# Late projections at every third round and output splits one per round, in the HGRN and attention stage of a hybrid decoder layer

## The chip, the cores and the metric

The kernel runs on one core of a Trainium2 chip. The metric is the device time of one execution, in microseconds (us); the time before is the median of 3 runs.

## The reference

One decoder layer over a sequence of 1024 tokens with width 1024, in float32. Features are kept as 8 blocks of 128 partitions, tokens along the free axis. Cut to what matters:

```python
def layer(h):
    a = rmsnorm(h) @ W_in                     # 30 blocks of 128 columns
    h = h + concat(hgrn2(a), dilated_window_mix(a), rwkv7(a)) @ W_out
    h = h + gated_mlp_with_causal_conv3(rmsnorm(h))
    h = h + sigmoid(rmsnorm(h) @ W_g) * (p @ W_p)
    return rmsnorm(h)

# hgrn2, four heads of 128: S_t = diag(f_t) S_{t-1} + (1 - f_t) i_t^T, o_t = S_t^T q_t,
#   then o * rsqrt(mean(o*o) + eps) * g * silu(gate)
# dilated_window_mix, four heads of 64: softmax attention over three dilated windows,
#   combined by their softmax denominators
# rwkv7, four heads of 64
```

## The kernel before

A float32 product is done as three matmuls of split operands, xh·whi + xl·whi + xh·wlo (`mm3`), where hi is the value rounded for TensorE's fast mode and lo is what is left. A weight block of 1024 columns is loaded, cast on ScalarE (whi, line 114) and subtracted on VectorE or GpSimd (wlo, line 116). `dense` runs the 8 blocks of the inner dimension through `mm3`.

The layer runs as stages: the norm, the RWKV heads in two pairs, then HGRN and attention together, the output projection, the MLP, the gate and the last norm. The engines' instruction order is static: a scheduler takes the instructions as the Python code issues them, with priorities, and writes one list for each engine.

The change touches the stage of HGRN and attention, which `phase_mix` writes. It interleaves five generators by a string of letters:

- A: HGRN heads 0 and then 2; B: HGRN heads 1 and then 3 (`handover`: the second begins when the first is 14 steps in).
- C: the attention (`swa`), two pairs of heads p of eight query blocks each: scores (swq on PE), mask and minimum (lg and sden on DVE), exponential on ACT, transposes (swt), values (swo) and their copy into the output tile ob.
- F: the late projections (`project_late`).
- M: what is left of the RWKV work.

There are 36 rounds. In each A has a turn, B from the sixth on, C in the rounds of `TURNS`, and F in the rounds of `LATE` (line 344). F has four blocks of W_in to project, 29, 18, 22 and 23, each in two halves of 512 tokens. A half is 24 matmuls of 128x512 into a PSUM tile zp, followed by its finish (the row scale at line 320, for some a sigmoid at line 460 and a product at line 462 into the tile zst) and a store to DRAM. The halves are called half 1 to half 8 below. When all are done, the buffers of the normalized input X are free, since nothing reads it any more: `project_late` takes tiles in the same buffers for the input of the output projection (`self.O`), and calls `o_split` for each block k in `self.done`, in one turn. A split is two casts on ScalarE (xh, line 160) and two subtractions (xl, line 162), the first half on DVE and the second on POOL. The blocks in `done` are 6, 7 (RWKV), 0, 1 (HGRN heads that have ended) and 4 (attention pair 0); blocks that come later are split by their own streams.

An HGRN head computes its scores by levels: a score matmul (hsc, line 989) gives what DVE selects into hS (line 991), DVE then rescales qt (line 1002), POOL or DVE rescales hk (line 1000), ACT copies ks (line 976), and the next level's hsc reads qt and ks. When a head ends, its output is squared and summed (hss, line 1066), POOL raises the sum to the power −0.5 (hrs, line 1069), DVE scales ho (line 1071), and PE transposes it (vt, line 1077).

Buffers that matter: the PSUM pool "mx" has four (zp, vt, swt, swo and hsc share it); the PSUM pool for scores has two (swq); zst has two, of which the attention's output tile ob of pair 0 holds one until it is split; the tag "sslot" of the attention's pool has four.

Of the kernel before, what the change touches and what calls it, by code (L numbers as in the profile page):

```python
# [10 lines left out]
F32 = mybir.dt.float32  # L11
# [7 lines left out]
P = 128  # L19
T = 1024  # L20
# [45 lines left out]
def interleave(order, streams):  # L66

    live = dict(streams)
    while live:
        for s in order:  # L70
            if s in live and next(live[s], STOP) is STOP:
                del live[s]
# [17 lines left out]
class Trunk:  # L90
# [231 lines left out]
    def phase_mix(self):  # L322
# [8 lines left out]
        with tc.tile_pool(name="hg", bufs=1) as slots, tc.tile_pool(name="sw", bufs=1) as sp:  # L331
# [8 lines left out]
            for r in range(36):  # L340
                order += "C" * (r in self.TURNS) + "A" + "B" * (r > 5) + "F" * (r in self.LATE)
            interleave(order, {"A": A, "B": B, "C": self.swa(sp), "F": self.project_late(self.rest), "M": self.more})

    LATE = (1, 3, 6, 9, 12, 15, 18, 20, 21)

    TURNS = [i * 33 // 22 for i in range(1, 23)]

# [116 lines left out]
    def project_late(self, js):  # L464


        nc = self.nc
        for j in js:
            w = self.load_w(self.a["w_in"][j])
            t = self.keep.tile([P, T], F32, tag="zst", name=self.nm("zst"), bufs=2)  # L470
            d = self.zpool.tile([P, T], F32, tag=f"z{j}", name=f"z{j}")
            kind = (j - 8) % 4 if j < 24 else 2
            turn = j < 24 and kind < 3
            for hf in (0, 1):
                ps = self.mxp.tile([P, HT], F32, tag="mx", name=self.nm("zp"))
                self.dense({hf: ps}, w, self.X, ND, halves=(hf,))
                dst = slice((hf ^ turn) * HT, ((hf ^ turn) + 1) * HT)
                r = self.R[:, hf * HT:(hf + 1) * HT]
                self.finish(kind, t[:, dst], *((ps[:, ::-1], r[:, ::-1]) if turn and hf else (ps, r)))
                nc.sync.dma_start(d[:, dst], t[:, dst])  # L480
                if hf:
                    self.z[j] = d
                yield
        self.O = self.xall()
        for k in self.done:
            self.o_split(k)

    def zload(self, j, pool_slot, eng=None):
        t = pool_slot("zl")
        (eng or self.nc.sync).dma_start(t, self.z[j])  # L490
        return t
# [680 lines left out]
    def swa_values(self, sp, d, qb, den, pT):  # L1172
        nc = self.nc
        if qb == 0:
            d["o"] = self.keep.tile([P, T], F32, tag="zst", name=self.nm("ob"), bufs=2)
        o = d["o"]
        po = self.mxp.tile([P, P], F32, tag="mx", name=self.nm("swo"))

        for kb in range(qb + 1):
            for h, hs in enumerate(self.HEADS):  # L1180
                nc.tensor.matmul(po[hs, :], d["V"][:, kb, hs], pT[h][:, kb * P:(kb + 1) * P], start=kb == 0, stop=kb == qb)
        nc.scalar.copy(o[:, qb * P:(qb + 1) * P], po)
        if qb % 4 == 3:
            nc.vector.reciprocal(den[:, :8], den[:, :8])
            return d, qb, o, den
# [627 lines left out]
```

## Time and profile before

| what | value |
|---|---|
| median of 3 runs | 1435.65 us (1434.49 to 1436.31) |
| profiled execution | 1436.1 us |
| its span | 1434.3 us |
| its mean granted TensorE clock | 0.989 |
| instructions | 22340 |
| HBM read, written | 119.76 MB, 46.40 MB |

The span is the time from the first to the last instruction of the profiled execution; 1.8 us of that execution lie outside it. Busy shares are shares of the span. In a timeline row stand the start, the duration, the engine, the line, the operation, the names of output and inputs, sizes, how many instructions were put together in the row, and in brackets the idle time of the engine before the row with what ended it. In a row of waits stand the total, the count and the longest. The granted clock is 1.00 at full speed.

### The profile page before, as it was taken

What the parts mean: (1) busy time and instruction counts of PE and PEld (TensorE: products, weight loads), DVE (VectorE), ACT (ScalarE), POOL (GpSimd) and SP (SyncE); (2) the same over time, 40 slices, a digit from 0 to 9 for tenths busy, and PEclk for the clock granted to TensorE, in tenths of its full rate; (3) what the DMA queues carried; (4) which work ended last, traced back from release to release, by engine and by line L of the source; (5) the groups of instructions that cost most, each with busy time, mean ns of one, the idle gap of its engine ahead of it and who ended that gap; (6) DMA issues with size and microseconds to landing.
All of it is one profiled execution on the core that took longest, in us unless ns stands there. A gap on an engine that the chain in (4) does not pass through costs nothing.

```text
span 1434.3 us, 22340 instructions
## 1 busy us (share of the span) xinstructions
PE 1392.4 (97%) x8642; PEld 1124.6 (78%) x8642; DVE 1063.9 (74%) x1629; ACT 603.6 (42%) x1015; POOL 391.7 (27%) x286
## 2 busy tenths in 40 slices
PE   8999999999999989999999999999999999999996
PEld 6768777777777867787788888888888888888885
DVE  7596353964657777458888888988898799777675
ACT  7411323123145475244544444344344444455542
POOL 5221011210122231121245445445453000002331
PEclk9999999999999999999999999999999999999998
DMA  6124111240442211652413232333223963451343
GB/s 219 45 81 118 61 50 56 81 119 31 153 141 104 84 50 46 241 192 96 147 74 111 96 110 96 110 110 110 101 98 134 351 235 105 122 148 45 133 158 114
DMA packets 80122, 167.61 MB, mean 117 GB/s; under 512 B 19984, under 2 KB 22288, under 8 KB 80016
## 3 DMA queue, kind: packets, MB, share of 16 engines
q1 hardware_dynamic: 66496, 146.52, 30.2%
q10 hardware_dynamic: 12656, 16.52, 3.3%
q0 software_dynamic: 864, 3.15, 0.6%
q8 instruction: 68, 1.11, 0.3%
q14 instruction: 38, 0.31, 0.1%
HBM read 119.76 MB, written 46.40 MB: 116 GB/s over the span
## 4 chain that ended last, share of the span: by engine, by line
PE 47%; issue 3%; DVE 2%; POOL 1%; ACT 1%; DMA 0%; POOLq 0%; ACTq 0%; DVEq 0%
PE bg L1300 16%; PE bv L1300 12%; PE bv L1594 7%; PE bg L1594 7%; PE dp L141 1%; PE dp L137 1%; PE dp L139 1%; POOL wlo L116 1%; PE bv L137 0%; PE bv L139 0%; PE bv L141 0%; DVE h L1690 0%; POOL xh L162 0%; ACT whi L114 0%; DVE gt L1689 0%
## 5 line engine op out<-in xcount | busy, mean ns | idle before, releaser
L137 PE MATMUL dp<-xh,whi 128*128 128x512 f32 x544 | 191.0, 411 | 6.2 <-DVE r L500 2.9
L139 PE MATMUL dp<-xl,whi 128*128 128x512 f32 x544 | 183.7, 397 | 0.5 <-DVE xl L411 0.5
L141 PE MATMUL dp<-xh,wlo 128*128 128x512 f32 x544 | 181.8, 395 | 0.0
L116 POOL TENSOR_TENSOR wlo<-wraw,whi 128x512 fp32r<-128x512 f32 x60 | 81.7, 1363 | 326.3 <-ACT whi L114 259.7
L116 POOL TENSOR_TENSOR wlo<-raw,whi 128x512 fp32r<-128x512 f32 x84 | 134.7, 1622 | 76.1 <-ACT whi L114 76.1
L114 ACT CAST whi<-wraw 128x512 fp32r<-128x512 f32 x120 | 73.0, 617 | 165.2 <-PE dp L139 113.1
L1300 PE MATMUL bg<-t,whi 128*128 128x512 f32 x352 | 133.2, 389 | 0.0
L137 PEld LDWEIGHTS dp<-xh,whi 128*128 128x128 f32 x544 | 100.2, 190 | 35.2 <-issue 6.8
L139 PEld LDWEIGHTS dp<-xl,whi 128*128 128x128 f32 x544 | 103.0, 190 | 24.0 <-DVE xl L411 1.0
L141 PEld LDWEIGHTS dp<-xh,wlo 128*128 128x128 f32 x544 | 103.3, 190 | 23.3 <-issue 0.8
L116 POOL TENSOR_TENSOR wlo<-s,whi 128x512 fp32r<-128x512 f32 x44 | 64.2, 1460 | 174.6 <-ACT whi L114 174.6
L1594 PE MATMUL bg<-t,whi 128*128 128x512 f32 x308 | 95.2, 390 | 0.0
L1594 PE MATMUL bv<-t,whi 128*128 128x512 f32 x308 | 94.8, 389 | 0.0
L114 ACT CAST whi<-raw 128x512 fp32r<-128x512 f32 x88 | 52.6, 619 | 94.6 <-issue 48.5
L114 ACT CAST whi<-s 128x512 fp32r<-128x512 f32 x66 | 38.9, 620 | 121.1 <-PE bg L1300 113.3
L1300 PEld LDWEIGHTS bg<-t,whi 128*128 128x128 f32 x352 | 66.0, 188 | 13.7
L190 POOL TENSOR_TENSOR rst<-rst,mhalf 128x4 f32<-128x4 f32 (+1 forms) x9 | 9.9, 1102 | 235.6 <-DVE rst L186 218.6
L1594 PEld LDWEIGHTS bv<-t,whi 128*128 128x128 f32 x308 | 57.8, 188 | 12.0
L1300 PE MATMUL bg<-t,wlo 128*128 128x512 f32 x176 | 67.2, 389 | 0.0
L1594 PEld LDWEIGHTS bg<-t,whi 128*128 128x128 f32 x308 | 57.7, 188 | 11.9
L1590 ACT CAST t<-t 128x512 fp32r<-128x512 f32 x77 | 47.8, 622 | 44.7 <-PE bv L1594 29.2
L116 DVE TENSOR_TENSOR wlo<-wraw,whi 128x512 fp32r<-128x512 f32 x60 | 47.6, 794 | 23.2 <-ACT whi L114 22.9
(417 smaller groups left out, 3422.9 us busy)
## 6 DMA issues: line engine op xcount, KB each, us to landing
raw<-in_ffn_up_dram SPq DMA_DIRECT2D x44, 512.0 KB, 3.4
wraw<-in_w_in_dram SPq DMA_DIRECT2D x28, 512.0 KB, 3.4
z<-zst SPq DMA_DIRECT2D x18, 512.0 KB, 2.8
gb<-ct SPq DMA_DIRECT2D x33, 256.0 KB, 2.3
t<-gb SPq DMA_DIRECT2D x33, 256.0 KB, 2.7
t<-gt SPq DMA_DIRECT2D x33, 256.0 KB, 2.7
zl<-z SPq DMA_DIRECT2D x16, 512.0 KB, 4.3
wraw<-in_ple_gate_dram SPq DMA_DIRECT2D x16, 512.0 KB, 3.4
```

Of the source, the lines that this page charges most:

```text
L114: self.cast = nc.scalar.copy(hi, src).ins
L116: eng.tensor_tensor(lo, src, hi.bitcast(F32), ALU.subtract)
L137: nc.tensor.matmul(ps[hf], wh, xh[hf], start=first, stop=False)
L139: nc.tensor.matmul(ps[hf], wh, xl[hf], start=False, stop=False)
L141: nc.tensor.matmul(ps[hf], wl, xh[hf], start=False, stop=last)
L190: nc.gpsimd.tensor_tensor(r2, r, self.mhalf[:, :n], ALU.pow)
L1300: nc.tensor.matmul(ps, w[part == 2][:, s], X[k][part == 1], start=start and k == part == 0, stop=k == 3 and part == 2, skip_group_check=no ...
L1590: nc.scalar.copy(xh, x)
L1594: nc.tensor.matmul(ps[m], wt[part == 2][:, m * P:(m + 1) * P], (xh, xl)[part == 1], start=k == part == 0, stop=k == NK - 1 and part == 2)
```

## The change

`LATE` gives the eight halves to the rounds 1, 4, 7, 10, 13, 16, 19 and 22 in place of 1, 3, 6, 9, 12, 15, 18 and 20. The splits, all in one turn at round 21 before, have the rounds 23 to 28, one each, by a `yield` behind each. The output tile ob of pair 1 is taken from the tag "sslot" and not from zst. The lines from 487 on move down by one, from 1177 on by two.

```diff
-    LATE = (1, 3, 6, 9, 12, 15, 18, 20, 21)
+    LATE = (1, 4, 7, 10, 13, 16, 19, 22, 23, 24, 25, 26, 27, 28)
...
         self.O = self.xall()
         for k in self.done:
             self.o_split(k)
+            yield
...
         if qb == 0:
-            d["o"] = self.keep.tile([P, T], F32, tag="zst", name=self.nm("ob"), bufs=2)
+            d["o"] = self.sp.tile([P, T], F32, tag="sslot", name=self.nm("ob"), bufs=4) if d["p"] else \
+                self.keep.tile([P, T], F32, tag="zst", name=self.nm("ob"), bufs=2)
```

The numbers of instructions on each engine stay the same. How they move is shown at three places. The first is PE between half 7 (zp_4943 before) and half 8 (zp_5040 before); hsc_4996 and hsc_5021 are two levels of the scores of one head. Before:

```order
L141 MATMUL zp_4943<-xh_119,wlo_4939 128x512
L1181 MATMUL swo_4982<-pT_4888,sV_4773 64x128
L1181 MATMUL swo_4982<-pT_4892,sV_4773 64x128
L1168 MATMUL swt_4987<-cst,lg_4882 128x128 x2
L1168 MATMUL swt_4992<-cst,lg_4885 128x128 x2
L1142 MATMUL swq_5069<-zl_4520,zl_4518 128x512 x2
L989 MATMUL hsc_4996<-qt_4653,ks_4908 64x64 x8
L1142 MATMUL swq_5183<-zl_4520,zl_4518 128x512
L1142 MATMUL swq_5183<-zl_4520,zl_4518 128x128
L989 MATMUL hsc_5021<-qt_4653,ks_5008 64x64 x8
L137 MATMUL zp_5040<-xh_89,whi_4933 128x512
L1142 MATMUL swq_5182<-zl_4520,zl_4518 128x512
```

The same place now, from the level ahead of half 7 (hsc_4955 now, zp_4992 is half 7) to the second level behind it:

```order
L1169 MATMUL swt_4951<-cst,lg_4885 128x128 x2
L990 MATMUL hsc_4955<-qt_4653,ks_4908 64x64 x8
L137 MATMUL zp_4992<-xh_105,whi_4982 128x512
...
L141 MATMUL zp_4992<-xh_119,wlo_4988 128x512
L990 MATMUL hsc_5021<-qt_4653,ks_4967 64x64 x8
L1143 MATMUL swq_5040<-zl_4520,zl_4518 128x512 x2
L1183 MATMUL swo_5049<-pT_4945,sV_4746 64x128
...
L1169 MATMUL swt_5056<-cst,lg_4934 128x128 x3
L1169 MATMUL swt_5062<-cst,lg_4937 128x128 x3
L990 MATMUL hsc_5067<-qt_4653,ks_5033 64x64 x8
```

Before, a few short rows stood between the two levels, and half 8 followed directly; now all of half 7 stands between them, and half 8 comes only after three more levels.

The second is DVE at the same place. Before, from the end of a head's output to the row of qt that the level hsc_5021 reads:

```order
L1066 TENSOR_REDUCE hss_5015<-hsq_5013 128x8
L1067 TENSOR_SCALAR hss_5015<-hss_5015 128x8
L1071 TENSOR_TENSOR ho_4911<-ho_4911,hrs_5018 128x1024
L938 TENSOR_SCALAR zl_5036<-zl_5036,olb,lb 128x1024
L320 TENSOR_TENSOR zp_4943<-zp_4943,rstd 128x512
L941 TENSOR_SCALAR hk_5112<-zl_5036 128x512 x2
L943 TENSOR_TENSOR qt_5115<-zl_5038,zl_5036 128x1024
...
L462 TENSOR_TENSOR zst_4941<-zst_4941,zp_4943 128x512
L991 COPY_PREDICATED hS_4701<-cmask,hsc_4996 128x4x64
L1002 TENSOR_TENSOR qt_4653<-qt_4653,hT_4703 128x2x32x8
```

The same place now:

```order
L992 COPY_PREDICATED hS_4701<-cmask,hsc_4955 128x4x64
L1003 TENSOR_TENSOR qt_4653<-qt_4653,hT_4703 128x2x32x8
L1067 TENSOR_REDUCE hss_4974<-hsq_4972 128x8
L1001 TENSOR_TENSOR hk_4650<-hk_4650,hT_4703 128x2x8x32
L1068 TENSOR_SCALAR hss_4974<-hss_4974 128x8
L162 TENSOR_TENSOR xl_5267<-zl_4524,xh_5266 128x512
L1072 TENSOR_TENSOR ho_4911<-ho_4911,hrs_4977 128x1024
L939 TENSOR_SCALAR zl_5036<-zl_5036,olb,lb 128x1024
L162 TENSOR_TENSOR xl_5275<-ob_3976,xh_5274 128x512
L320 TENSOR_TENSOR zp_4992<-zp_4992,rstd 128x512
L992 COPY_PREDICATED hS_4701<-cmask,hsc_5021 128x4x64
L1003 TENSOR_TENSOR qt_4653<-qt_4653,hT_4703 128x2x16x16
```

The selection hS and the qt of the same level stood behind the head's output, the next head's gate and the finish of half 7; now they stand ahead of them.

The third is ACT behind half 8 (zp_5040 before, zp_5180 now), where the casts of the splits, the sigmoid of half 8's finish and copies out of PSUM share one queue. Before:

```order
L160 CAST xh_5129<-zl_4524 128x512
L114 CAST whi_5897<-wraw_5895 128x512
L160 CAST xh_5137<-ob_4003 128x512
L1182 COPY ob_4981<-swo_4982 128x128
L160 CAST xh_5141<-oc_1813 128x512
L114 CAST whi_5901<-wraw_5895 128x512
L160 CAST xh_5143<-oc_3441 128x512
L460 ACT_TABLE_LOAD
L460 ACTIVATE zst_4941<-zp_5040 128x512
L1182 COPY ob_4981<-swo_5078 128x128
```

Now:

```order
L160 CAST xh_5250<-zl_4524 128x512
L977 COPY ks_5247<-hk_5083 128x2x128x2
L160 CAST xh_5252<-zl_4970 128x512
L114 CAST whi_5897<-wraw_5895 128x512
L160 CAST xh_5258<-ob_3976 128x512
L160 CAST xh_5262<-oc_1813 128x512
L114 CAST whi_5901<-wraw_5895 128x512
L160 CAST xh_5264<-oc_3441 128x512
L460 ACT_TABLE_LOAD
L460 ACTIVATE zst_4990<-zp_5180 128x512
L1019 COPY hV_5209<-vt_5210 128x512
L1019 COPY hV_5209<-vt_5216 128x512
```

The casts are still in a row, though their turns are spread over six rounds; the copies of head 3's transposes (hV) now follow directly behind the sigmoid. On PE the transposes vt_5210, vt_5216 and vt_5223, four swq rows and then vt_5229, which waits for ACT, stand behind half 8.

## The prediction

> **What bounds the kernel now.** I read the page first (the span, the busy shares, the granted clock), then the windows over the end of the HGRN and attention stage, then the waits of TensorE there, then the timelines of PE, DVE and ACT over the one stretch that stands out.
>
> The page, its first line and its first two parts:
>
> ```profile
> span 1434.3 us, 22340 instructions
> ...
> PE 1392.4 (97%) x8642; PEld 1124.6 (78%) x8642; DVE 1063.9 (74%) x1629; ACT 603.6 (42%) x1015; POOL 391.7 (27%) x286
> ...
> PEclk9999999999999999999999999999999999999998
> ```
>
> TensorE is busy 97% of the span, at nearly full clock. So an edit that moves matmuls without removing any can gain only what PE idles, and what it runs at a lowered clock, near the place of the edit. The whole idle is 1434.3 − 1392.4 = 41.9 us over all stages. The windows of the stage's end (columns: window, length, busy time and rows of PE, PEld, DVE, ACT, POOL, then granted clock, DMA share, GB/s) say where:
>
> ```profile
> 470.00:505.00 35.00, 35.00 (x370) 29.50 (x370) 26.98 (x61) 19.00 (x43) 8.22 (x7) 1.00 0.27 91
> 505.00:525.00 20.00, 16.44 (x88) 10.87 (x85) 13.31 (x26) 11.17 (x19) 6.67 (x6) 0.83 0.12 40
> 525.00:542.00 17.00, 15.85 (x208) 13.07 (x206) 15.06 (x33) 14.13 (x31) 6.46 (x6) 1.00 0.16 51
> 542.00:590.00 48.00, 44.18 (x419) 36.46 (x415) 31.01 (x58) 21.88 (x40) 10.04 (x8) 1.00 0.18 63
> 590.00:660.00 70.00, 69.44 (x313) 57.39 (x312) 42.20 (x63) 30.08 (x52) 15.76 (x12) 1.00 0.60 220
> ```
>
> Up to 505 us PE has no idle at all; from 505 to 525 it loses 3.56 us and its clock falls to 0.83; 525 to 542 loses 1.15 more; 542 to 590 loses 3.82; after that it is full again. The waits of PE between 400 and 590 us (in total, times, longest):
>
> ```profile
> PE hsc L989 <- DVE qt L1002: 3.4, 2, 3.0
> PE vt L1077 <- DVE ho L1071: 3.0, 2, 1.8
> PE hsc L963 <- ACT ob L1182: 1.2, 1, 1.2
> PE swq L1142 <- DVE sden L1152: 0.6, 1, 0.6
> PE hpo L1059 <- DVE hst L1047: 0.2, 1, 0.2
> ```
>
> The largest is one wait of 3.0 us of an HGRN score matmul (hsc) for DVE's rescaled qt. PE's timeline around it (start, duration, row, idle before it); the row at 498.00 is the first of half 7 of the late projections, 503.64 the first behind that half, and 511.18 the first of half 8:
>
> ```profile
> 498.00 0.47 PE L137 MATMUL zp<-xh,whi 128*128 128x512 f32 x1
> ...
> 503.64 0.44 PE L1181 MATMUL swo<-pT,sV 128*64 128x128 f32 x4
> ...
> 506.27 1.34 PE L1142 MATMUL swq<-zl,zl 64*128 64x512 f32 x4
> 510.57 0.69 PE L989 MATMUL hsc<-qt,ks 128*64 128x64 f32 x16 [2.96 <-DVE qt L1002]
> 511.18 0.50 PE L137 MATMUL zp<-xh,whi 128*128 128x512 f32 x1
> 511.62 2.03 PE L1142 MATMUL swq<-zl,zl 64*128 64x512 f32 x4
> ...
> 515.02 0.63 PE L139 MATMUL zp<-xl,whi 128*128 128x512 f32 x1
> 515.45 0.63 PE L141 MATMUL zp<-xh,wlo 128*128 128x512 f32 x1
> ...
> 521.52 0.66 PE L1181 MATMUL swo<-pT,sV 128*64 128x128 f32 x8
> ...
> 523.58 2.30 PE L1142 MATMUL swq<-zl,zl 64*128 64x512 f32 x8 [0.60 <-DVE sden L1152]
> ...
> 531.12 1.15 PE L963 MATMUL hsc<-zl,hk 128*64 128x64 f32 x32 [1.15 <-ACT ob L1182]
> ...
> 542.21 2.72 PE L1142 MATMUL swq<-zl,zl 64*128 64x512 f32 x8
> ...
> 584.23 0.95 PE L1077 MATMUL vt<-cst,ho 128*128 128x128 f32 x7 [1.79 <-DVE ho L1071]
> ```
>
> After 2.96 us of idle the same kind of matmul starts 0.43 us after the one before it (515.02 to 515.45); half 7's 24 rows, from 498.00 to 503.64, start every 0.235 us. A three-microsecond window inside half 8 shows what the clock was, and the trace's other large waits tell from where on a gap costs clock:
>
> ```profile
> 513.60:516.60 3.00, 3.00 (x8) 2.42 (x8) 1.74 (x3) 0.62 (x1) 1.55 (x2) 0.50 0.00 0
> 360.00:365.00 5.00, 2.75 (x11) 1.91 (x11) 4.28 (x14) 0.92 (x3) 0.00 (x0) 0.69 0.57 210
> 715.00:720.00 5.00, 4.53 (x19) 3.45 (x20) 4.77 (x6) 0.85 (x3) 2.88 (x2) 1.00 0.33 105
> ...
> 362.25 0.48 PE L876 MATMUL pS<-S,MG 64*64 64x64 f32 x4 [2.38 <-DVE MG L862]
> ...
> 715.15 0.47 PE L1300 MATMUL bg<-tp3h,whi 128*128 128x512 f32 x1 [1.95 <-ACT whi L114]
> ```
>
> A gap of 2.38 us lies in a window at 0.69; the gap of 1.95 us left its window at 1.00, as 1.79 us did that from 542 to 590. So in this trace the price of a gap jumps somewhere between 1.95 and 2.38 us; I work with the middle, about 2.1 (an estimate from these rows).
>
> Why DVE is late is in its own timeline:
>
> ```profile
> 503.93 1.22 DVE L1071 TENSOR_TENSOR ho<-ho,hrs 128x1024 f32<-128x1024 f32 x1 [1.75 <-POOL hrs L1069]
> 505.07 0.81 DVE L938 TENSOR_SCALAR zl<-zl,olb,lb 128x1024 f32<-128x1024 f32 x1
> ...
> 508.81 0.68 DVE L462 TENSOR_TENSOR zst<-zst,zp 128x512 f32<-128x512 f32 x1
> 509.40 0.43 DVE L991 COPY_PREDICATED hS<-cmask,hsc 128x256 f32<-128x256 uint8 x1
> 509.74 0.69 DVE L1002 TENSOR_TENSOR qt<-qt,hT 128x512 f32<-128x512 f32 x1
> ```
>
> From 503.93 to 509.40 DVE works without a pause at things the next score matmul does not need: the output scaling of the head that ends (ho), the next head's gate (zl, hk, qt), the finish of half 7 (scale and zst). The two rows it needs, hS and qt, stand behind them.
>
> **The change part by part.** No instruction is added or dropped on any engine, so busy time stays: the sum is over idle and clock alone.
>
> *The halves one round later.* Half 7 now stands between the hsc row ahead of it and the hsc row that had waited, and DVE's queue has hS and qt right behind their hsc, ahead of ho. So the chain that took DVE 509.74 + 0.69 − 503.93 = 6.5 us now runs beside half 7's 5.64 us of PE work plus the short rows. The 2.96 us go. With them goes the slow clock: half 8 and its four swq rows take 521.52 − 511.18 = 10.34 us; undisturbed they would take 5.64 + 1.34 = 6.98, so 3.36 us come back. The 0.60 (swq for DVE, which was finishing half 8 and masking) and the 1.15 (hsc L963 for ACT, which was behind on its casts) are in rows that now stand ahead of half 8 and with other work before them: 1.75 us. The 0.20 of hpo, further ahead, has the halves at other places around it and goes too. Together 2.96 + 3.36 + 1.75 + 0.20 = 8.27 us at most.
>
> *The Trainium skill on this clock.* The Trainium skill, page "TensorE: Matmul & The Clock Gate", Part 1 (The HAM clock gate), says that the array runs at half rate after about 3.4 us of idle in a free-running window, and again at full rate after about that long of work. The trace agrees on the half (0.50) but shows it after 2.96 and in a window with a gap of 2.38 us, so here the measured rows decide.
>
> *New waits.* PE meets four new places where the order makes it wait; the trace of before has none of them. Three are short ones: a zp row that needs a PSUM buffer just given back, an hsc row behind a longer list of DVE work, and a swq row whose score buffer DVE must have masked. The nearest rows are the waits of 0.2 and 0.60 above; I take 0.43 each, 1.3 in all, from 0 to 1.8. The fourth is behind half 8. There the transposes of head 3 need a PSUM buffer that ACT frees by copying the first of them out, and ACT has this queue behind half 8 in the trace of before (the copies of L1018 came later there):
>
> ```profile
> 522.80 0.62 ACT L160 CAST xh<-oc 128x512 fp32r<-128x512 f32 x1
> 523.43 1.28 ACT L460 ACT_TABLE_LOAD   x1
> 524.73 0.60 ACT L460 ACTIVATE zst<-zp 128x512 f32<-128x512 f32 x1
> ...
> 532.93 1.07 ACT L1018 COPY hV<-vt 128x512 f32<-128x512 f32 x2 [0.25 <-PE vt L1017]
> ```
>
> If one cast is left when half 8 ends, ACT frees the buffer after 0.62 + 1.28 + 0.60 + 0.53 = 3.0 us; with two and a weight cast left, as before (the table load at 523.43 came 1.9 us behind half 8's end at 521.5), after 1.9 + 1.28 + 0.60 + 0.53 = 4.3. PE has twelve transposes to do meanwhile (0.95 / 7 = 0.136 us each by the row at 584.23, 1.6 together) and four swq rows, two of them half as long as those at 506.27 (1.34 for four, so 1.0): 2.6 us. So it waits 0.4 to 1.7; I take 1.35. Behind PE's waiting row stand hsc, swo and swt of the last pair; they wait with it. All new waits: 2.65 us, from 0.4 to 3.5.
>
> *The splits one per round.* Five splits of two casts each (0.62 us on ACT) with subtractions on DVE and POOL. Only the order of issue changes; the scheduler still puts four casts in a row on ACT behind half 7 and again behind half 8, because what they write was the operand of those halves. Cost on the path: nothing beyond the fourth wait above, which contains it. What hides them is the last part of the stage, 542 to 660, where ACT is busy 21.88 of 48 and 30.08 of 70 us. If that cover went, ten casts would be 6 us.
>
> *The output tile of the second pair* takes a slot of another pool. It is taken when pair 1 begins, and the slot is free since that pair's v was transposed. No copy, no new wait: nothing, up to one short wait (0.2), within the bound above.
>
> *What follows.* From the swq at 542.21 on the rows of PE, DVE and ACT stand as before; the waits in that part, 1.2 and 1.79 us the longest (the row of vt), are chains from one engine to the next and shift along. 590 to 660 is 99% busy, so what is gained ahead of it reaches the end. The sum: −8.27 + 2.65 = −5.62 us. Against the profiled execution of 1436.1 us (span 1434.3, 1.8 outside) this gives 1430.5; the median of the runs shown is 0.45 lower, hence 1430.0.
>
> **The rivals.**
>
> *The gap comes back behind half 8.* ACT's burst of casts, table load and copies is the one place where my wait comes near the jump: 4.3 − 2.6 = 1.7 against 2.1. For it: ACT is busy 14.13 of 17 us in the stretch 525 to 542, so a little lateness adds up. Against: the casts become free during half 8, not after it. It would cost a gap of about 2.5 and again 3.36 of clock instead of 1.35: −8.27 + 1.3 + 5.86 = −1.1, about 1434.5. Chance 0.16.
>
> *DVE becomes the bound of the thin stretch (slower).* Between half 7 and half 8, and again behind half 8, all PE rows are short and each needs something of DVE; in 525 to 542 DVE is already busy 15.06 of 17 us. Half 8 was the block that covered DVE there, and it now stands later. If DVE falls behind by more than 2.1 us in both halves of that stretch, each gap costs 2.5 + 3.36: −8.27 + 0.9 + 2 × 5.86 = +4.35, about 1440.0. Against: half 7 takes up the longest chain. Chance 0.13. It decides from the point where a second gap passes 2.1 us.
>
> *The slow clock stays.* The clock might not hang on this gap but on when the chip samples it, or on the thin rows before. Then only the waits go: −2.96 − 1.75 − 0.20 + 2.65 = −2.3, about 1433.4. By the Trainium skill's page named above, whose idle window is longer than the 2.96 us gap, this is the outcome to expect; the trace, which has no full-clock gap above 1.95 us, speaks against it. Chance 0.08.
>
> *Swallowed later.* The stage's tail is a chain of two heads through DVE and POOL; if it is started by a load and not by PE, part of the gain turns into longer waits at 559 and 584 us. PE's 44.18 of 48 us there leaves room for about half: 1433 or so. Chance 0.08.
>
> That the change does not do what it says holds for the casts (they stay bunched), which is in the sum already.
>
> **How the numbers follow.** The forecast has the remaining 0.55. A measurement of this kernel tells about 0.2%, 2.9 us, from no change, so faster is below about 1432.8 and slower above 1438.5. Faster: the forecast, less a little for new waits at their upper end, and the edges of the third and fourth rival, 0.53 + 0.04 + 0.04 = 0.61. Slower: the second rival and a bad case of the first, 0.16. Same: 0.23. The range begins where nearly no new wait appears (−8.27 + 0.4 = −7.9, so 1427.8 at the median; a little less, 1427.2, since the runs shown differ by 1.8) and reaches beyond the first rival, to 1436.0; outside lie the slower cases and little else.
>
> **What would show it.** In the changed kernel's profile the wait hsc <- qt of 2.96 must be gone, the window of half 8 must stand at 1.00 and half 8 take 5.6 us, and the waits of PE between 400 and 545 us must add up to about 2.7 with none above 2.1. A window below 1.00 between 500 and 545 would make the prediction wrong by over 3 us; waits at 560 to 590 longer than 1.2 and 1.8 would show the gain swallowed; a clock of 0.5 without a gap before it would show the third rival.

## The result, and the profile after

| kernel | median us | lowest to highest | executions | ratio to before, 95% interval |
|---|---|---|---|---|
| before | 1435.07 | 1432.68 to 1436.31 | 4 | |
| changed, first time | 1425.91 | 1425.31 to 1426.41 | 4 | 0.9935 [0.9923, 0.9948] |
| changed, again (experiment) | 1428.12 | 1426.31 to 1429.74 | 6 | 0.9948 [0.9936, 0.9960] |
| changed, once more (experiment) | 1427.78 | 1425.98 to 1430.49 | 6 | 0.9940 [0.9922, 0.9958] |

The change makes the kernel faster by 0.5 to 0.7%. The forecast was 1430.0 us in a range of 1427.2 to 1436.0; the first median lies 1.3 us below the range, the two later ones inside it. Why they differ is part of what follows. The interval of each ratio lies below 1.

The page of the changed kernel, the same lines as were shown of before:

```profile
span 1424.6 us, 22342 instructions
...
PE 1381.9 (97%) x8642; PEld 1118.0 (78%) x8642; DVE 1066.8 (75%) x1629; ACT 602.5 (42%) x1015; POOL 392.5 (28%) x286
...
PEclk9999999999999999999999999999999999999998
```

The span is 9.7 us shorter, and PE's busy time is 10.5 us shorter, though it has the same 8642 matmuls. A lowered clock lengthens the matmuls that run under it, so busy time holds what the prediction had counted as clock, and the total alone does not tell whether it holds more. The windows over the end of the stage (the same columns as in the prediction):

```profile
505.00:525.00 20.00, 17.31 (x156) 12.82 (x154) 19.27 (x34) 16.71 (x34) 11.25 (x9) 1.00 0.12 40
525.00:542.00 17.00, 16.98 (x180) 13.32 (x180) 15.31 (x39) 13.57 (x26) 2.95 (x3) 1.00 0.26 79
542.00:590.00 48.00, 44.56 (x382) 37.38 (x379) 26.61 (x45) 16.08 (x29) 11.34 (x9) 1.00 0.43 160
```

The granted clock is 1.00 where it was 0.83. DVE is now busy 19.27 of 20 us and POOL 11.25, against 13.31 and 6.67. The waits of PE between 400 and 545 us in the changed kernel:

```profile
PE vt L1024 <- ACT hV L1019: 2.4, 1, 2.4
PE hsc L990 <- DVE qt L1003: 0.6, 1, 0.6
PE zp L137 <- DVE pT L1170: 0.5, 1, 0.5
PE swt L1169 <- DVE hS L992: 0.2, 1, 0.2
PE zp L137 <- ACT hV L1019: 0.2, 1, 0.2
```

The 3.0 us of hsc for qt are gone, and so are the 1.2, 0.6 and 0.2; a wait of 2.4 us and four short ones have come (a fifth of 0.12 us is too short for this view). To see what the stretch as a whole gained, take two marks that stand at the same place of PE's order in both kernels, the first scores of the attention and the transposes of ho near the end. Before:

```profile
401.07 0.49 PE L1142 MATMUL swq<-zl,zl 64*128 64x128 f32 x4
...
558.98 1.06 PE L1077 MATMUL vt<-cst,ho 128*128 128x128 f32 x8 [1.18 <-DVE ho L1071]
```

and after:

```profile
398.43 0.49 PE L1143 MATMUL swq<-zl,zl 64*128 64x128 f32 x4
...
549.16 1.06 PE L1078 MATMUL vt<-cst,ho 128*128 128x128 f32 x8 [1.18 <-DVE ho L1072]
```

From mark to mark it took 157.91 us before and 150.73 after: 7.18 us less. The 2.64 us by which the first mark already comes earlier lie ahead of anything that the change moves: up to there PE has the same rows in both. The section on the prediction comes back to them.

The 7.18 us, by the trace: the waits between the marks are 2.96 + 1.15 + 0.60 + 0.35 + 0.20 = 5.26 before, and 2.41 + 0.59 + 0.55 + 0.16 + 0.15 + 0.12 = 3.98 after, without the 1.18 that both have: 1.3 us less. The two windows at half rate before, 6.8 us, did 3.4 us of work: 3.4 less. That leaves 2.5 us which the prediction's sum doesn't have. The row group that shortened by as much are the score matmuls. Of these rows alone (tile swq), the windows from the first mark to the last give, before and after, length, busy time of PE and count, clock, DMA share, GB/s:

```profile
401.00:560.00 159.00, 24.57 (x96) 0.98 0.23 77
```

```profile
398.00:551.00 153.00, 21.14 (x96) 1.00 0.24 81
```

The same 96 matmuls take 3.43 us less. 0.69 of that is the slow clock (2.03 against 1.34 us for four of them in the prediction's rows), 2.7 are something else (what is over the 2.5 was lost in other rows). Two blocks show it. The first scores of query block 4 of the first pair, before (DVE's mask of the block ahead of it, then PE's matmuls):

```profile
421.64 0.68 DVE L1152 CUSTOM_DVE_ANT_0 lg<-swq,swmask 128x512 f32<-128x512 f32 x1
...
421.83 1.91 PE L1142 MATMUL swq<-zl,zl 64*128 64x512 f32 x8
```

and the same block after, where DVE had masked the block ahead long before:

```profile
412.44 0.69 DVE L1153 CUSTOM_DVE_ANT_0 lg<-swq,swmask 128x512 f32<-128x512 f32 x1
...
418.91 1.35 PE L1143 MATMUL swq<-zl,zl 64*128 64x512 f32 x8
```

Eight rows of two heads took 1.35 us; four of one head alone took 1.34 (the row at 506.27 in the prediction's timeline). So the two heads' matmuls, which use 64 of the 128 rows of the array each, run at the same time when both can start. Before, the first head's started at 421.83, but the second head's buffer came free only when DVE's mask ended (421.64 + 0.68 = 422.32). The matmuls ran one head behind the other for 0.56 us. None of this is idle time of PE, and so no view of waits has it. With the halves at other places there are 9 us between the two blocks in place of 3, and DVE is done.

### The profile page after: what moved, and what is told of

It is laid out like the page before. It is cut to its first block, busy times and chain, and to the rows that moved or that the text cites. A ratio compares the mean times of both kernels' runs of the same rounds, so it can differ in the third digit from the quotient of the medians.

```text
span 1424.6 us, 22342 instructions
## 1 busy us (share of the span) xinstructions
PE 1381.9 (97%) x8642; PEld 1118.0 (78%) x8642; DVE 1066.8 (75%) x1629; ACT 602.5 (42%) x1015; POOL 392.5 (28%) x286
## 3 DMA queue, kind: packets, MB, share of 16 engines
q0 software_dynamic: 864, 3.15, 0.6%
## 4 chain that ended last, share of the span: by engine, by line
PE 48%; issue 3%; DVE 2%; POOL 1%; ACT 1%; DMA 0%; POOLq 0%; ACTq 0%; DVEq 0%
PE bg L1302 16%; PE bv L1302 12%; PE bv L1596 7%; PE bg L1596 7%; PE dp L141 1%; PE dp L137 1%; PE dp L139 1%; POOL wlo L116 1%; PE bv L137 0%; PE bv L139 0%; PE bv L141 0%; DVE h L1692 0%; POOL xh L162 0%; DVE gt L1691 0%; ACT whi L114 0%
```

## The experiments

Each has its ratio to the kernel before on the same chip. What each leaves or adds in the computation is said with its edit; where nothing is said, it computes the same.

**The changed kernel with the splits in one turn** (late_burst).

```diff
-    LATE = (1, 4, 7, 10, 13, 16, 19, 22, 23, 24, 25, 26, 27, 28)
+    LATE = (1, 4, 7, 10, 13, 16, 19, 22, 23)
...
             self.o_split(k)
-            yield
```

> The changed kernel with all splits in one turn again (round 23). Theory: the halves' rounds carry the whole gain and the spread of the splits none, since the order of PE and ACT comes out the same: 1426 us, within 1.5 us of the changed kernel. Rival: the spread relieves ACT behind half 8; then without it the wait of vt for ACT grows above 2.4 us and the time is 1428.5 or more.

Median 1429.02 us (1426.22 to 1432.60, 11 executions), ratio 0.9961 [0.9947, 0.9975]. PE's and ACT's order are row for row those of the changed kernel, and the wait behind half 8 is again 2.4 us, not longer: the rival's cause is not there, though the time is in its range. Spreading the splits over the rounds leaves ACT's queue as it is. But the median is 3 us above the 1426 expected, 1 to 3 us above those of the changed kernel at an equal order, and the executions spread by 6 us. In the profiled executions the stretch between the two marks is the same to 0.04 us (150.77 us here), so the difference arises outside it. That asked for the next runs.

**The old rounds with the splits spread** (old_halves), and **the new rounds alone** (late_only).

```diff
-    LATE = (1, 4, 7, 10, 13, 16, 19, 22, 23, 24, 25, 26, 27, 28)
+    LATE = (1, 3, 6, 9, 12, 15, 18, 20, 21, 22, 23, 24, 25, 26)
```

```diff
-    LATE = (1, 3, 6, 9, 12, 15, 18, 20, 21)
+    LATE = (1, 4, 7, 10, 13, 16, 19, 22, 23)
```

The first edit is against the changed kernel, the second against the kernel before.

> The halves at the rounds of before (1, 3, 6, ... 20), the splits one per round from 21 on, and the output tile moved. Theory: nothing gained, 1435 us within 1.5, with the wait of 3.0 us of hsc for qt and a half-rate window behind it still there. Rival (the spread of the splits carries a third or more of the 9.2 us): 1432 or less.

> The halves at the rounds of after, nothing else: splits in one turn, output tile of the second pair in zst as before. Theory: 1426 to 1427 us, the tile costs at most a short wait (0.2 to 1 us). Rival: without the other slot the tile and block 23 fight for the two zst buffers, half 7 is late and PE waits 2 us or more: 1428.5 or more.

The old rounds: 1433.71 us (12 executions), ratio 1.0000 [0.9988, 1.0011], and the waits of before are there, but for the 1.2 us for ACT:

```profile
PE hsc L990 <- DVE qt L1003: 3.0, 1, 3.0
PE swq L1143 <- DVE sden L1153: 0.6, 1, 0.6
PE hpo L1060 <- DVE hst L1048: 0.2, 1, 0.2
```

Between the marks its profiled execution took 155.61 us, 2.3 less than before; the ratio of the executions shows no such gain.

The new rounds alone: 1428.92 us (11 executions), ratio 0.9958 [0.9944, 0.9972]. This is 2 to 3 us above what was expected and not told apart from late_burst. The time is in the rival's range, but its wait of 2 us or more is not there: the longest between the marks is 0.7 us, and the stretch takes 151.69 us against 150.73. The wait of 2.4 us behind half 8 is gone, and the score matmuls take 22.25 us against 21.14. So the old slot gives another order behind half 8 and costs about 1 us there in this execution. The rounds carry the gain; what the spread of the splits and the other slot give, these executions can't tell from nothing.

**Only halves 7 and 8 late** (last_two), and **only halves 2 to 6 late** (half8_20).

```diff
-    LATE = (1, 4, 7, 10, 13, 16, 19, 22, 23, 24, 25, 26, 27, 28)
+    LATE = (1, 3, 6, 9, 12, 15, 19, 22, 23, 24, 25, 26, 27, 28)
```

```diff
-    LATE = (1, 4, 7, 10, 13, 16, 19, 22, 23, 24, 25, 26, 27, 28)
+    LATE = (1, 4, 7, 10, 13, 16, 18, 20, 23, 24, 25, 26, 27, 28)
```

> The changed kernel with halves 2 to 6 at the rounds of before and only halves 7 and 8 late (19, 22). Theory: the gap of 3.0 us and its slow clock go, and the score matmuls of the second attention pair run side by side more often, but those of the first pair do not (1.3 us): 1427.3 us, from 1426 to 1429. Rival 1: only the gap and its clock make the gain, the rest is chance; then it is the same as the changed kernel, 1426. Rival 2: the early halves carry a third or more: 1430 or more.

> Halves 2 to 6 one round later as in the changed kernel, halves 7 and 8 at the rounds of before (18 and 20), splits one per round. In the order half 7 and half 8 stand around the two score levels as before. Theory: the wait of 3.0 us for qt and the half-rate window behind it come back; what the early halves give (score matmuls of the first attention pair side by side, 1.3 us, and 0.2 of idle) stays: 1433.5 us, from 1432 to 1435. Rival (the early halves carry the gain): 1430 or less.

last_two: 1431.18 us (12 executions), ratio 0.9979 [0.9967, 0.9990], 4 us above the 1427.3 expected. The number is that of rival 2, but the profile gives another reason. The old gap is gone, but two new waits of 1.7 and 1.6 us stand close to each other:

```profile
PE swt L1169 <- DVE hS L992: 1.7, 1, 1.7
PE vt L1024 <- ACT hV L1019: 1.6, 1, 1.6
PE swo L1183 <- DVE zst L462: 0.7, 1, 0.7
```

and in the profiled execution 6.8 us at half rate follow them. half8_20: 1432.45 us (12 executions), ratio 0.9984 [0.9972, 0.9996], 1 us below the 1433.5 expected. The gap is back (3.15 us), with 10.2 us at half rate behind it. By the ratios each part alone gives 2 to 3 us, both together 7 to 9.

**The gap filled, in the kernel before** (before_fill): useless matmuls into the PSUM tile that the next ones overwrite. They stand ahead of the score level before the one that had waited.

```diff
             sc = mxp.tile([P, 4, 64], F32, tag="mx", name=self.nm("hsc"))
+            if h == 2 and l == 4:
+                for i in range(20):
+                    nc.tensor.matmul(sc[:, 0:2, :].rearrange("p c i -> p (c i)"), self.ident, self.ident, start=True, stop=True)
```

> The kernel before with 20 useless 128x128 matmuls (2.7 us) ahead of a score matmul, where TensorE came to wait 3.0 us for qt; one pair of swq rows also comes together again in the order. Nothing else moves. Theory: DVE ends qt at the same time, but PE is busy until then, the half-rate window behind is gone, and half 8 takes 5.6 us in place of 9 to 10: 1431 us, from 1430 to 1433, with no wait less on DVE's side. Rival 1 (the slow clock comes from the thin rows and not from the gap): half 8 stays slow and the time is 1435 or more. Rival 2 (the 3 us of waiting are what costs): 1435.

1431.71 us (12 executions), ratio 0.9977 [0.9966, 0.9988]: the time is as the theory has it. PE over the place, from the added rows to the first of half 8 and the first row behind it:

```profile
506.35 4.73 PE L987 MATMUL hsc<-cst 128*128 128x128 f32 x40
511.01 0.69 PE L992 MATMUL hsc<-qt,ks 128*64 128x64 f32 x16
...
513.76 0.69 PE L992 MATMUL hsc<-qt,ks 128*64 128x64 f32 x16 [0.78 <-DVE qt L1005]
514.37 0.50 PE L137 MATMUL zp<-xh,whi 128*128 128x512 f32 x1
...
520.04 0.66 PE L1184 MATMUL swo<-pT,sV 128*64 128x128 f32 x8
```

The added rows took 4.73 us and not 2.7, the second hsc starts at 513.76 where it started at 510.57 (0.7 us of this lie ahead of the first mark), and still the kernel is faster: half 8 takes 520.04 − 514.37 = 5.7 us, at full clock. So the slow clock hung on the gap and not on the thin rows, which are still there. What the idle time itself cost, this run does not tell, since the gap was filled and not shortened. Two things give the gain: the clock, 3.4 us, and the pair's swq rows, which run together again, 1.3 us.

**The two heads' matmuls in another order** (after_unpaired), one head's two blocks and then the other's.

```diff
-            for b in range(0, nk, HT):
-                w = min(HT, nk - b)
-                for h in (1, 0):
+            for h in (1, 0):
+                for b in range(0, nk, HT):
+                    w = min(HT, nk - b)
```

> The changed kernel with the two heads' score matmuls issued one head after the other where a head has two of them (blocks 4 to 7 of each pair), in place of in turn. Theory (two score matmuls that use different halves of the array's rows run at the same time when they stand next to each other): each such block takes up to twice its 1.3 to 1.9 us, 10 us in all, of which part falls into waits that are there anyway: 6 to 11 us slower than the changed kernel. Rival (order within a block is of no account, the same columns are streamed): within 1.5 us of it.

1426.87 us (4 executions), ratio 0.9948 [0.9928, 0.9968]: no slower than the changed kernel. The theory fell as it was put: where the rows of the two heads stand next to each other, their order is of no account, and in the trace both heads start within 0.02 us of each other all the same. What kept them apart in the block shown above is a wait of the second head for its buffer, which this kernel doesn't have more of.

**The changed kernel again** (after_again), and **with two waits filled** (fill_two).

```diff
+                    if self.fillp == 1 and t == 12:
+                        for _ in range(20):
+                            nc.tensor.matmul(pS, self.ident, self.ident[:, :64], start=True, stop=True)
...
+            if h == 3 and hf == 0:
+                for _ in range(2):
+                    nc.tensor.matmul(pt, self.ident, self.R[:, :HT], start=True, stop=True)
```

> The changed kernel itself, unaltered, in more executions. Theory (half-rate windows come and go from execution to execution, with where a gap falls between fixed borders 3.4 us apart): the executions spread over 1425 to 1432 us, like those of the kernel with the splits in one turn, with a median near 1428.5; the four first executions were on the low side. Rival (the spread of the splits gives 3 us): all near 1426.

> The changed kernel with useless matmuls ahead of two waits of TensorE: 20 small ones into the pS tile where it waits 2.4 us for DVE at 361 us, and two of 512 columns ahead of the wait of 2.4 us at 524 us. They write PSUM that the next matmul overwrites; the result is unchanged. Theory (a window of 3.4 us that is less than half busy is followed by one at half rate): no half-rate window near 361 or 524 us in any execution, median 1 to 2 us below the changed kernel and the slowest executions gone. Rival (the clock does not follow busy time): same time, or 1 to 2 us slower where the added matmuls outlast the wait.

The changed kernel came out at 1428.12 us and spread over 3.4 us, so the first four were on the low side, as the theory says. The filled one was 1438.36 us (11 executions), ratio 1.0017 [1.0008, 1.0026], and tells nothing of the clock. The first fill waited for the same thing as the row behind it and ran after the wait:

```profile
362.08 6.87 PE L879 MATMUL pS<-cst 128*128 128x64 f32 x40 [2.38 <-DVE MG L864]
```

The second went to the wrong head (571 us): the transposes at 524 us are those of head 2, which the prediction and the text ahead of it called head 3.

**The fill put right** (fill_right), and **the changed kernel once more** (after_more).

```diff
+        if self.fillp == 1 and g == 2:
+            for _ in range(4):
+                nc.tensor.matmul(py[0], self.ident, self.R[:, :192], start=True, stop=True)
...
+            if h == 2 and hf == 0:
+                for _ in range(2):
+                    nc.tensor.matmul(pt, self.ident, self.R[:, :HT], start=True, stop=True)
```

> The changed kernel with useless matmuls that run inside the two long waits and not behind them: four of 192 columns ahead of the pyo rows before the wait at 361 us, and two of 512 columns ahead of the first transposes of hk before the wait at 524 us, in PSUM tiles that are free at that time and overwritten after. Theory (a window of 3.4 us that is less than half busy makes the next one half rate): both waits shrink by what was put in, no half-rate window stands behind them, and the executions spread less: none above 1429, median 0.5 to 1.5 us below the changed kernel in the same call. Rival (the spread has other causes): the same spread, median the same or 1 us later.

> The changed kernel again, on the same chip as the one with the useless matmuls. Theory: median 1427 to 1429 us with single executions up to 1431; profile with the 2.4 us gaps at 361 and 524 us, and half rate behind one of them or none, by where the gap falls between the borders. Rival: all executions near 1426 as in the first four.

fill_right: 1430.80 us (12 executions), ratio 0.9972 [0.9959, 0.9984], slower than the changed kernel. Both waits shrank, to 1.1 and 0.7 us, and no half-rate window stood behind them; but the scheduler put a rescaling of hk, three rows of hT and a second mask on DVE ahead of a head's hS and qt, and a new wait came:

```profile
PE swt L1176 <- DVE hS L996: 2.9, 1, 2.9
PE vt L1031 <- ACT hV L1023: 0.7, 1, 0.7
```

with its own half-rate window. Eleven of the twelve lie within 2.1 us, one 4 us above: less spread, but this run can't separate that from its new gap. after_more: 1427.78 us (6 executions), 1425.98 to 1430.49, as expected.

**Half 8 one round earlier** (half8_21) **or two later** (half8_24), against the changed kernel.

```diff
-    LATE = (1, 4, 7, 10, 13, 16, 19, 22, 23, 24, 25, 26, 27, 28)
+    LATE = (1, 4, 7, 10, 13, 16, 19, 21, 23, 24, 25, 26, 27, 28)
```

```diff
-    LATE = (1, 4, 7, 10, 13, 16, 19, 22, 23, 24, 25, 26, 27, 28)
+    LATE = (1, 4, 7, 10, 13, 16, 19, 24, 25, 26, 27, 28, 29, 30)
```

> The changed kernel with half 8 one round earlier (21). Two score levels that stood ahead of half 8 now stand behind it. Theory: the wait of vt for ACT behind half 8 (2.4 us) shrinks below 1.5 us, since other PE work now covers ACT's casts, and nothing else moves: 1 us below the changed kernel, 1427 us. Rival: the two levels ahead of half 8 covered DVE; without them a wait of 1 us or more for DVE takes its place: same or slower.

> The changed kernel with half 8 two rounds later (24), behind the transposes of head 3. Theory: the transposes no longer wait for ACT behind half 8, so the wait of 2.4 us goes, but PE has no long block between half 7 and there, so 1 to 3 us of waits for DVE come in its place: 1427 to 1429 us. Rival: such a gap passes 2 us together with its neighbours inside one 3.4 us window and half-rate windows appear there: 1431 or more.

1429.22 us (7 executions), ratio 0.9957 [0.9941, 0.9972], and 1428.48 us (5 executions), ratio 0.9948 [0.9935, 0.9960]. Both take the 2.4 us wait away; half8_24 has 1.3, 0.9 and 0.9 us in its place, half8_21 two of 0.9 us. In the profiled executions the stretch between the marks is as long as in the changed kernel within 0.6 us. Neither beats it, and these executions tell no difference: the late rounds are flat around this choice.

## Why the prediction was wrong, point by point

**The step that failed** is "the sum is over idle and clock alone". It followed from "No instruction is added or dropped on any engine, so busy time stays". Busy time did not stay: the score matmuls of two heads run side by side or not, by when DVE frees the second buffer. That term, 2.5 us, was put at nothing; it was in no row of waits and stood in the mean duration of the swq rows, which I did not compare from block to block. It was read from the traces and not isolated, since the experiment made for it (the order of the rows) did not separate the heads. A second term at nothing was the clock ahead of the stretch, 2.64 us in this execution (below). Both shortened the time. By the stretch alone, 7.18 us where the sum has 5.62, it would have come to about 1428.5, inside the range and near the two later medians; the 2.64 us ahead of the stretch took it below.

**The gap and its clock** were right. 2.96 us of waiting went, and half 8 runs at full clock; it takes 519.16 − 513.57 = 5.6 us; the removed slow time is 3.4 us (forecast 3.36). The waits of 0.60, 1.15 and 0.20 went too. before_fill shows that the clock hung on the gap. The third rival, that the slow clock stays, did not come true here.

**The new waits** were mis-sized: 3.98 us in all, against 2.65 and a bound of 3.5. The three short ones are five, 1.57 us together (forecast 1.3, bounds 0 to 1.8). The fourth, on the transposes of head 2 and not of head 3, is 2.41 us, outside its bounds of 0.4 to 1.7. I had taken ACT for the last in the chain; ACT was ready at 522.27 and waited for DVE:

```profile
520.99 1.28 ACT L460 ACT_TABLE_LOAD   x1
523.40 0.60 ACT L460 ACTIVATE zst<-zp 128x512 f32<-128x512 f32 x1 [1.13 <-DVE zp L320]
```

```profile
517.73 1.67 DVE L162 TENSOR_TENSOR xl<-oc,xh 128x512 fp32r<-128x512 f32 x1
519.33 1.77 DVE L162 TENSOR_TENSOR xl<-zl,xh 128x512 fp32r<-128x512 f32 x1
521.02 1.75 DVE L116 TENSOR_TENSOR wlo<-wraw,whi 128x512 fp32r<-128x512 f32 x1
522.68 0.69 DVE L320 TENSOR_TENSOR zp<-zp,rstd 128x512 f32<-128x512 f32 x1
```

Three subtractions stand ahead of the scale of half 8, and each took about 1.7 us in place of the 0.69 that such a row takes alone. In these us POOL ran the other halves' subtractions without a pause. Two of its rows, and, from the kernel before, a DVE row beside which POOL was idle:

```profile
520.50 1.72 POOL L162 TENSOR_TENSOR xl<-ob,xh 128x512 fp32r<-128x512 f32 x1
522.18 1.71 POOL L162 TENSOR_TENSOR xl<-oc,xh 128x512 fp32r<-128x512 f32 x1
...
499.78 0.69 DVE L162 TENSOR_TENSOR xl<-zl,xh 128x512 fp32r<-128x512 f32 x1 [2.25 <-ACT xh L160]
```

So the casts bunched behind half 8 did cost, by way of DVE and POOL slowing each other, which the prediction had put at nothing. Without ACT's 1.13 us of waiting for DVE the fourth wait would have been about 1.3 us (an estimate: 2.41 − 1.13), close to the 1.35 taken. The Trainium skill, page "SBUF — State Buffer", section "SBUF: two separate sides", says that a DVE instruction with two inputs in SBUF and a GpSimd instruction that reads SBUF take turns at a shared pair of ports, and that the later one waits for the whole instruction of the other. The trace agrees that they hold each other up, with 1.7 against 0.69 us on DVE; full turns would take 0.69 + 1.30 = 1.99 us (a POOL row of before that ran while DVE was idle took 1.30), and 1.7 is less.

**The jump at 2.1 us** was wrong. The new gap of 2.41 us left the clock at 1.00, and the gap of 2.38 us at 361 us cost clock before and none after. The trace of before also has a gap of 2.07 us, at 94 us, with half rate behind it; I had not read it. What decides is read from a grid of 3.41 us, on which the clock changes of an execution fall. Before, two pairs of a window with a gap and what follows it:

```profile
358.50:361.90 3.40, 1.36 (x50) 0.86 (x49) 3.32 (x10) 1.41 (x4) 0.00 (x0) 1.00 0.47 153
361.90:365.30 3.40, 3.05 (x11) 1.94 (x12) 2.75 (x9) 0.00 (x0) 0.00 (x0) 0.51 0.39 160
508.70:512.10 3.40, 1.53 (x18) 1.06 (x19) 3.40 (x10) 2.07 (x6) 0.00 (x0) 1.00 0.22 82
512.10:518.90 6.80, 6.80 (x17) 4.82 (x16) 3.24 (x6) 1.52 (x3) 2.83 (x2) 0.50 0.16 40
```

and after:

```profile
356.40:359.80 3.40, 2.22 (x54) 1.58 (x52) 3.40 (x10) 1.06 (x2) 0.00 (x0) 1.00 0.27 78
359.80:363.20 3.40, 2.20 (x13) 1.57 (x14) 2.92 (x11) 0.46 (x3) 0.00 (x0) 1.00 0.58 235
520.30:523.70 3.40, 1.82 (x12) 0.78 (x9) 3.07 (x3) 2.25 (x4) 3.40 (x3) 1.00 0.00 0
523.70:527.10 3.40, 2.57 (x39) 2.23 (x40) 3.07 (x6) 3.38 (x6) 3.10 (x3) 1.00 0.28 58
```

Of these, a window in which PE is busy 1.36 or 1.53 of 3.40 us is followed by one or two at half rate; one with 1.82 or more is not. Of the gap of 2.38 us, 2.0 lay in one window before, and 1.2 in each of two after. Where the borders lie against the kernel's start differs from one execution to the next. The Trainium skill, page "TensorE: Matmul & The Clock Gate", Part 1 (The HAM clock gate), has a free-running window of about 3.4 us, and the trace agrees with 3.41; it has a whole window of idle for the drop, where here 1.9 us of idle in 3.4 were enough.

**The first four executions** are low for the same reason as far as the traces tell. The 2.64 us by which the first mark came earlier are mostly two such windows of before, behind gaps of 2.07 and 2.38 us that the changed kernel has too. Their cost comes and goes: the profiled executions of before, old_halves, before_fill and late_burst have the window behind the gap at 361 us, those of the changed kernel not. The gap of 2.07 us shows it within the changed kernel, first in after_more and then in the first execution:

```profile
91.90:95.30 3.40, 1.33 (x6) 0.86 (x5) 3.05 (x4) 2.62 (x4) 0.00 (x0) 1.00 0.53 81
95.30:98.70 3.40, 3.40 (x7) 1.94 (x7) 3.40 (x7) 0.66 (x2) 1.27 (x1) 0.50 0.00 0
```

```profile
90.20:93.60 3.40, 2.55 (x12) 1.77 (x10) 2.05 (x3) 1.13 (x2) 0.00 (x0) 1.00 0.97 215
93.60:97.00 3.40, 2.18 (x7) 1.19 (x8) 3.40 (x4) 1.54 (x3) 1.28 (x1) 1.00 0.00 0
```

Where it costs clock, the first mark comes at 400.04 us, where not, at 398.43; from mark to mark both take 150.73 us. The forecast had no term for it and a range too narrow at its low end by that. One such window, 1.6 us by the two marks, covers most of the 2 us between the medians of the changed kernel. That this explains all of it, and that no such window stood in the other three of the first four, is argued and not shown: those have no trace, and fill_right, which was to settle it, brought a gap of its own.

**The rest** came as forecast: with the new rounds the splits' spread moves nothing in PE's and ACT's order, the tile's other slot costs nothing that shows, and what is gained reaches the end, where the same waits of 1.18 and 1.8 us for ho remain.

## What to carry to other kernels

An edit that moves blocks without removing any can gain in busy time too: compare the mean duration of the same matmuls from place to place, since two that use half of the array's rows each run at once only if both have their buffer. Price a gap of TensorE by how much of it can fall into one 3.4 us window and not by its length alone, and take that price as a chance per execution. Two medians of a few executions each can differ by such a window, so compare the stretch that the edit moves as well. Where several copies or subtractions come due together on DVE and POOL, use the duration that they have beside each other, not the one alone.

## What the runs showed of the hardware

The order of two heads' matmuls that stand next to each other in PE's queue does not matter for whether they overlap: one head's blocks first and then the other's gave the same 0.9948. Over all profiled executions up to 1408 us, by PE's busy share of the full-clock windows of the 3.41 us grid, half rate came after every window that was less than 0.42 busy, after 6 of 18 from 0.43 to 0.50, and above that at three places only (0.57 in last_two, 0.61 to 0.69 near 664 us in eight executions, 0.61 ahead of the added rows of fill_two), for which these runs show no reason. A DVE subtraction of 128x512 took 0.69 us alone and 1.67 to 1.77 us beside POOL's.
